# One fused three-block kernel: early expert blocks taken evenly over the experts, dense weights stored by eight blocks, six gathers held, one-hots scaled on ScalarE and GpSimd

## The chip, the cores and the metric

The kernel runs on one core of one Trainium2 chip. The metric is the device time of one execution, in microseconds; lower is better. The engines have names of their own in the trace: PE is TensorE's matmul (PEld its weight load), DVE is VectorE, ACT is ScalarE, POOL is GpSimd, SP is SyncE, which here only issues DMAs.

## The reference, cut to what matters

The program is one transformer-like block (attention and a feed-forward part) followed by a second block whose last part is a product-key mixture of experts. Only that last part is touched. It has 512 tokens of width 1024 and 16384 experts, each a row of `u_tab` and a row of `v_tab`; every token picks 16 experts in each of 8 heads.

```python
def block(hb):
    n = hb.shape[0]
    q = (hb @ w_q).reshape(n, PEER_HEADS, 2, PEER_HALF)
    s = jnp.einsum('nhid,hikd->nhik', q, sub_keys).astype(jnp.float32)
    s_top, i_top = lax.top_k(s, PEER_TOPK)
    cand = s_top[:, :, 0, :, None] + s_top[:, :, 1, None, :]
    cand_idx = i_top[:, :, 0, :, None] * PEER_N_KEYS + i_top[:, :, 1, None, :]
    best, pos = lax.top_k(cand.reshape(n, PEER_HEADS, PEER_TOPK * PEER_TOPK), PEER_TOPK)
    idx = jnp.take_along_axis(cand_idx.reshape(n, PEER_HEADS, -1), pos, axis=-1)
    w = jax.nn.softmax(best, axis=-1)
    u = jnp.take(u_tab, idx, axis=0)
    act = jax.nn.gelu(jnp.einsum('nhkd,nd->nhk', u, hb).astype(jnp.float32))
    out = jnp.einsum('nhk,nhkd->nd', w * act, jnp.take(v_tab, idx, axis=0))
    return out.astype(hb.dtype)
```

## The kernel before, in words

The kernel splits the tokens of this part in two. The first 192 (`NS`) are done as written: 128 expert rows for each token are gathered, a row of `u_tab` is multiplied with the token and summed, a row of `v_tab` is weighted and summed. The other 320 (`ND`) are done densely: for each of 128 *blocks* of 128 experts TensorE multiplies the block's part of `u_tab` with the tokens, ScalarE takes gelu, VectorE multiplies with a matrix W of routing weights that is zero where a token did not pick an expert, and TensorE multiplies with the block's part of `v_tab`. Matrix operands are split in a high and a low half (`split`: ScalarE rounds, VectorE subtracts), and three matmuls make one product (`mm3`, 320 columns each). Weights come in slabs of 1 MB (`raw`, two buffers `wr`, issued by SP), two blocks to a slab of `u_s`.

Three stages in a row are touched.

*Routing* (1700 to 1960 us; the loop `for u in range(16)`). TensorE makes scores (`scores`), VectorE finds the 16 best (`top16`), GpSimd adds candidates (`cd`), and `decode(p)` turns positions into expert numbers for two heads at a time. Beside it TensorE makes 30 *early* blocks (`s_block32`: eight matmuls in plain fp32, then gelu). 38 blocks are early: the first 22 (`NACT`) stay in SBUF, the last 16 (`NSPILL`) go to DRAM (`Sd`) and come back when used.

*One-hots* (1960 to 2104 us; the loop `for sb in range(ND // SB)`, 20 times 16 tokens). For four tokens at a time VectorE compares an iota with the two key numbers (`A`, `B`, tiles of four 128x128 one-hots), `B` is scaled by the routing weights, TensorE multiplies `B` and `A` to the 128x128 matrix of W of each token, and ScalarE copies it to `stg`, which SP stores to DRAM (`Wd`) once for each 16 tokens. In the loop and behind it stand the last early blocks, eight in all.

*Dense* (2104 to 3084 us; the loop `for g in range(NG)`, 32 groups of four blocks). W is loaded for eight blocks at a time (`w_load`). `s_block` makes a fresh block (`pg`, 24 matmuls), `ahead` makes more at a rate of 0.86 a block, so that activations lie some twenty blocks ahead, until block 112, where the spilled ones begin. A group ends in 96 matmuls with `v_s` (`acc`) and eight additions to `x`.

Through all three runs the generator `spa = sparse()`, the work of the first 192 tokens. Each call gathers one row for each of 128 partitions (`rows`, an indirect DMA on GpSimd's queue, seven buffers `ro`), and before that, when three gathers are outstanding (`GLAG`), uses the oldest: a *u row* by a dot product on VectorE (L1337), a *v row* by waiting until four are there and then eight matmuls (`pv`, L1371). 192 u rows and 192 v rows come in the order of `mixed`. It is called 57 times in routing, 20 times in the one-hot stage, and at a rate of 0.82 (`GATHERS`) at 12 places of each group. The order on each engine is that of the code, as a scheduler arranges it; a queue works strictly in its order.

## Time and profile before

| | us |
|---|---|
| median of 3 runs | 3109.74 |
| lowest and highest run | 3103.26, 3118.66 |
| the profiled execution's own time | 3101.83 |
| its span, first to last instruction | 3100.0 |
| PE busy | 2899.0 |
| VectorE busy | 1989.1 |
| ScalarE busy | 1195.9 |
| GpSimd busy | 537.1 |

The runs time the program as a whole; the profile is one execution of it, and the views below are all of that one. Busy times overlap between engines and are a mean over stages with different limits. A busy PE is not PE at its peak, since matmuls are pipelined and their ends are modelled: how many matmul records end in a stretch says more.

### The profile page before, as it was taken

How to read it: one execution, taken by the hardware profiler on the slowest of the kernel's cores; microseconds unless marked ns; L12 is line 12 of the kernel's file. 1: busy time of each engine (PE TensorE's matmuls, PEld its weight loads, DVE VectorE, ACT ScalarE, POOL GpSimd, SP SyncE). 2: the span in 40 equal slices, each digit the busy share in tenths (PEclk: the TensorE clock that was granted, in tenths of full speed). 3: DMA queues.
4: the chain of work that ended last, by engine and by line, in shares of the span. 5: the costliest groups of instructions: out<-in, count | busy, mean ns of one | idle time of the engine just before them, and what ended most of it. 6: DMA issues, size and time to landing. Idle time of an engine off the chain costs nothing.

```text
span 3100.0 us, 43712 instructions
## 1 busy us (share of the span) xinstructions
PE 2899.0 (94%) x17230; PEld 2406.1 (78%) x17230; DVE 1989.1 (64%) x3987; ACT 1195.9 (39%) x1950; POOL 537.1 (17%) x447
## 2 busy tenths in 40 slices
PE   7999999999999999999999997589899989999987
PEld 4786588888898887888887765478888878888866
DVE  4755557554587677444446889997876666654554
ACT  3644445443364433344323110583333333333322
POOL 0000000000000000000000457312434434333332
PEclk9999999999999999999999998799999999999998
DMA  6203422222222232221122558479888888788895
GB/s 239 68 28 115 171 96 83 95 95 95 84 94 96 82 107 75 99 69 55 68 100 73 169 220 300 170 268 317 320 307 307 304 291 293 270 320 310 310 341 215
DMA packets 161806, 551.68 MB, mean 178 GB/s; under 512 B 14512, under 2 KB 70576, under 8 KB 124352
## 3 DMA queue, kind: packets, MB, share of 16 engines
q1 hardware_dynamic: 104416, 343.87, 31.7%
q0 software_dynamic: 55296, 201.35, 18.0%
q10 hardware_dynamic: 1888, 3.66, 0.3%
q8 instruction: 135, 2.21, 0.3%
q14 instruction: 71, 0.58, 0.1%
HBM read 522.98 MB, written 25.82 MB: 177 GB/s over the span
## 4 chain that ended last, share of the span: by engine, by line
PE 72%; DVE 11%; DMA 7%; ACT 4%; issue 3%; POOL 2%; SPq 0%; DVEq 0%; ACTq 0%; POOLq 0%
PE pg L129 15%; PE pg L133 15%; PE pg L132 15%; PE acc L129 4%; PE acc L133 3%; PE acc L132 3%; PE pv L1371 3%; DMA wr<-in_v_s_dram 2%; DMA ro<-in_u_r_dram,idxU 2%; DVE ro L1337 2%; DVE wl L104 2%; PE w L1601 1%; ACT B L1596 1%; ACT stg L1602 1%; PE yq L1041 1%
## 5 line engine op out<-in xcount | busy, mean ns | idle before, releaser
L104 DVE TENSOR_TENSOR wl<-wr,wh 128x1024 fp32r<-128x1024 f32 x446 | 548.9, 1235 | 520.6 <-ACT wh L103 491.5
L129 PE MATMUL pg<-ah,wh 128*128 128x512 f32 (+3 forms) x2472 | 859.4, 348 | 12.2 <-ACT wh L103 4.4
L133 PE MATMUL pg<-ah,wl 128*128 128x512 f32 (+3 forms) x2472 | 852.6, 345 | 8.5 <-DVE wl L104 8.3
L132 PE MATMUL pg<-al,wh 128*128 128x512 f32 (+3 forms) x2472 | 852.4, 345 | 0.0
L103 ACT ACTIVATE wh<-wr 128x1024 fp32r<-128x1024 f32 x446 | 469.2, 1058 | 911.4 <-PE pg L132 467.8
L129 PEld LDWEIGHTS pg<-ah,wh 128*128 128x128 f32 x2472 | 468.6, 190 | 82.7 <-ACT ac L1428 9.3
L133 PEld LDWEIGHTS pg<-ah,wl 128*128 128x128 f32 x2472 | 467.8, 190 | 63.2 <-DVE wl L104 11.7
L132 PEld LDWEIGHTS pg<-al,wh 128*128 128x128 f32 x2472 | 468.6, 190 | 53.1 <-issue 4.0
L129 PE MATMUL acc<-gh,wh 128*128 128x320 f32 x1024 | 325.3, 319 | 38.2 <-DVE x L1678 33.9
L133 PE MATMUL acc<-gh,wl 128*128 128x320 f32 x1024 | 321.2, 315 | 8.4 <-DVE wl L104 8.4
L1328 POOL DMA_INDIRECT ro<-in_u_r_dram,idxU x192 | 251.1, 1308 | 446.9 <-DVE dots L1337 324.2
L132 PE MATMUL acc<-gl,wh 128*128 128x320 f32 x1024 | 321.5, 314 | 0.0
L1337 DVE CUSTOM_DVE_ANT_0 ro<-ro,hT 128x1024 f32<-128x1024 f32 x192 | 234.6, 1249 | 52.6 <-DMA ro<-in_u_r_dram,idxU 52.5
L1328 POOL DMA_INDIRECT ro<-in_v_r_dram,idxV x192 | 208.7, 1087 | 325.1 <-PE pv L1371 239.7
L129 PEld LDWEIGHTS acc<-gh,wh 128*128 128x128 f32 x1024 | 197.2, 193 | 75.6 <-issue 53.3
L133 PEld LDWEIGHTS acc<-gh,wl 128*128 128x128 f32 x1024 | 197.4, 193 | 9.6 <-DVE wl L104 9.5
L1197 POOL MEMSET att<- 128x512 f32 x4 | 2.0, 524 | 1163.6 <-DVE mx L1119 1050.1
L132 PEld LDWEIGHTS acc<-gl,wh 128*128 128x128 f32 x1024 | 197.3, 193 | 0.0
L1441 PE MATMUL pg<-h,wr 128*128 128x320 f32 x608 | 171.7, 438 | 8.0 <-DMA wr<-in_u_s_dram 8.0
L1441 PEld LDWEIGHTS pg<-h,wr 128*128 128x128 f32 x608 | 115.4, 193 | 54.3 <-DMA wr<-in_u_s_dram 8.8
L1678 DVE TENSOR_TENSOR x<-x,acc 128x320 f32<-128x320 f32 x256 | 111.6, 483 | 13.5 <-PE acc L133 12.3
L1601 PE MATMUL w<-A,B 128*128 128x128 f32 x640 | 95.3, 299 | 26.5 <-ACT B L1596 24.5
(570 smaller groups left out, 3892.8 us busy)
## 6 DMA issues: line engine op xcount, KB each, us to landing
wr<-in_u_s_dram SPq DMA_DIRECT2D x64, 1024.0 KB
wr<-in_v_s_dram SPq DMA_DIRECT2D x64, 1024.0 KB
wr<-in_w_in_dram SPq DMA_DIRECT2D x40, 1024.0 KB
wr<-in_w_up_dram SPq DMA_DIRECT2D x22, 1024.0 KB
Wd<-stg SPq DMA_DIRECT2D x20, 1024.0 KB
W<-Wd SPq DMA_DIRECT2D x64, 320.0 KB
wr<-in_ada_w_dram SPq DMA_DIRECT2D x16, 1024.0 KB
wr<-in_w_inA_dram SPq DMA_DIRECT2D x12, 1024.0 KB
```

The lines of the kernel that those rows point to most:

```text
L103: S.activation(hi, src, AF.Copy)
L104: eng.tensor_tensor(lo, src, hi.bitcast(F), op=OP.subtract)
L129: ins = TE.matmul(ps, lh, rh, start=first, stop=False)
L132: TE.matmul(ps, lh, rl, start=False, stop=False)
L133: TE.matmul(ps, ll, rh, start=False, stop=last)
L1041: TE.matmul(pq[:, b * 128 + f * 64:b * 128 + f * 64 + 64], St[:, b * 128:b * 128 + 128], Cf[:, 16 + c * 64:80 + c * 64], start=True, stop= ...
L1328: G.indirect_dma_start(out=t, out_offset=None, in_=a[table], in_offset=bass.IndirectOffsetOnAxis(ap=idx, axis=0))
L1337: yield "u_r", idxU[:, j:j + 1], lambda t, j=j: pin(V.tensor_tensor_reduce(t, t, hx, scale=1.0, scalar=0.0, op0=OP.mult, op1=OP.add, accum ...
L1371: ins = TE.matmul(pv[hf][32 * q:32 * q + 32], sel[:, q], ts[q][:, hf * 512:hf * 512 + 512], start=(i == 0), stop=(i == n - 1))
L1441: TE.matmul(ps, slab[-1][:, c:c + 128], h32[:, k], start=(k == 0), stop=(k == 7))
L1601: last = TE.matmul(ps[:, :, t], B[:, t], A[:, t], start=True, stop=True)
L1678: V.tensor_add(x, x, acc[dc])
```

## The change

The early blocks are no longer the first 22 and the last 16: 19 slabs are taken at even distances over the 64 (`eslab`). The sixteen blocks of the last eight of them are made first and go to DRAM, the 22 others stay in SBUF (`kept`). The dense loop asks `act(n)` for each block, three ahead of use: a kept one, a load, or a fresh one, in small new buffers. `ahead` and the pinned order of its matmuls are gone. The three first rounds of routing make no early block now (26 blocks in routing, seven in the one-hot loop, five behind it; in the order that TensorE gets, one of the seven stands behind too).

`Wd` is laid out by groups of eight blocks, so that a partition's load is one run of 2560 bytes, no longer five of 512; the store in the one-hot stage writes sixteen runs of 512 bytes, formerly one of 8192.

`sparse` uses a row when gathers and held v rows together reach six. Its calls move: 40 in routing, 10 in the one-hot loop, 0.875 a place in the dense loop, and what is left before the last group's matmuls. 20 u rows of the first 128 tokens, not 60, precede those of the other 64, and a round of four v rows has seven u rows, not five.

All of `B` is compared at once. ScalarE scales two of four one-hots, formerly three; GpSimd scales two; VectorE's one fused compare and scale is gone. The last decode runs on VectorE alone, as do the last head's candidate sums.

```diff
-GLAG = 3
-
-GATHERS, SPACE = 0.82, 0.86
+GATHERS = 0.875
...
     def mixed():
         u1, v2 = first(range(128), hT), second(range(128, 192), 128, 16)
-        yield from islice(u1, 60)
+        yield from islice(u1, 20)
         yield from first(range(128, 192), hT2)
         for _ in range(16):
             yield from islice(v2, 4)
-            yield from islice(u1, 5)
+            yield from islice(u1, 7)
...
-            if len(flying) == GLAG:
+            while len(flying) + len(held) >= NRO - 1:
                 t, u = flying.pop(0)
                 u(t)
...
-        Wd = dw.tile([ND // SB, 128, 128, SB], F, name="Wd")
+        Wd = dw.tile([128 // WE, 128, ND // SB, WE, SB], F, name="Wd")
...
-        early = chain(range(128 - NSPILL, 128), range(NACT))
+        def act(n, pool):
+
+            if n in kept:
+                return kept[n]
+            ac = pool.tile([128, ND], F, name="ac", tag="ac")
+            if n in enum:
+                SY.dma_start(ac, Sd[enum[n] - NACT])
+            else:
+                S.activation(ac, gemm_one(ust, hd), AF.Gelu_apprx_tanh)
+            return ac
+
+
+        eslab = [(2 * i + 1) * 64 // (NACT + NSPILL) for i in range((NACT + NSPILL) // 2)]
+        enum = {2 * b + j: 2 * i + j for i, b in enumerate(eslab) for j in range(2)}
+        fresh = [b for b in range(64) if b not in eslab]
+        todo = sorted(enum, key=lambda n: (enum[n] + NSPILL) % (NACT + NSPILL))
...
-                    E = V if p == 3 and b else G
+                    E = V if p == 3 else G
...
-                for _ in range(2 if u < 15 else 0):
+                for _ in range(2 if 2 < u else 0):
                     s_block32()
-                for _ in range(6 if u > 8 else 5 if u > 5 else 0):
+                for _ in range(5 if 5 < u < 14 else 0):
                     next(spa)
...
+                CE = V if hh == 7 else G
...
-                next(spa)
+                if sb % 2:
+                    next(spa)
...
-                    for t in range(3):
+                    for t in (0, 1):
                         S.activation(B[:, t], B[:, t], AF.Copy, scale=wl(t))
-                    V.tensor_scalar(B[:, 3], iot, i2T[:, t0 + 3:t0 + 4], wl(3), op0=OP.is_equal, op1=OP.mult)
+                        G.tensor_scalar(B[:, t + 2], B[:, t + 2], wl(t + 2), None, op0=OP.mult)
...
-                SY.dma_start(Wd[sb], stg)
-                if sb % 5 == 1 and len(acts) < NACT - 4:
+                SY.dma_start(Wd[:, :, sb].rearrange("g p e t -> p g e t"), stg.rearrange("p (g e) t -> p g e t", e=WE))
+                if sb % 3 == 1 and len(todo) > 4:
...
-                SY.dma_start(Wn[-1][:, c], Wd[c, :, n:n + WE].rearrange("s p e t -> p s e t"))
+                SY.dma_start(Wn[-1][:, c], Wd[n // WE, :, c])
...
-                    while len(acts) <= min(n + 2, 127):
-                        if len(acts) < 128 - NSPILL:
-                            s_block()
-                        else:
-                            s_load()
+                    while len(acts) <= min(n + 3, 127):
+                        acts.append(act(len(acts), pact2))
...
-                    ahead()
+                if g == NG - 1:
+                    for _ in spa:
+                        pass
```

The order of instructions shows what the diff alone does not, at three places. The first is TensorE at the end of routing, where the early blocks (`pg` from `wr`) stand ahead of the transposes of the expert numbers (`i1T`, `i2T`, `wT`). Before:

```order
L1441 MATMUL pg<-h_13137,wr 128x320 x2
L1490 MATMUL sc<-skT,qT 128x128 x4
L1441 MATMUL pg<-h_13137,wr 128x320 x62
L1581 MATMUL i1T<-con,i_13446 128x128 x4
L1581 MATMUL i2T<-con,i_13447 128x128 x4
L1581 MATMUL wT<-con,ww 128x128 x4
```

And now:

```order
L1452 MATMUL pg<-h_13137,wr 128x320 x2
L1496 MATMUL sc<-skT,qT 128x128 x4
L1452 MATMUL pg<-h_13137,wr 128x320 x78
L1590 MATMUL i1T<-con,i_13446 128x128 x4
L1590 MATMUL i2T<-con,i_13447 128x128 x4
L1590 MATMUL wT<-con,ww 128x128 x4
```

Sixteen more of these matmuls, two blocks, lie between the last scores and the transposes, though routing has four blocks fewer in all.

The second place is the one-hot loop. VectorE before, for four tokens and the next dot product (L1337):

```order
L1592 TENSOR_TENSOR A<-iot,i1T 128x512
L1592 TENSOR_TENSOR B<-iot,i2T 128x384
L1597 TENSOR_SCALAR B<-iot,i2T,wlT 128x128
L1592 TENSOR_TENSOR A<-iot,i1T 128x512
L1592 TENSOR_TENSOR B<-iot,i2T 128x384
L1597 TENSOR_SCALAR B<-iot,i2T,wlT 128x128
L1337 ISA ro,dots<-ro,hT 128x1024
```

VectorE now:

```order
L1602 TENSOR_TENSOR B<-iot,i2T 128x512
L1602 TENSOR_TENSOR A<-iot,i1T 128x512
L1602 TENSOR_TENSOR B<-iot,i2T 128x512
L1602 TENSOR_TENSOR A<-iot,i1T 128x512
L1602 TENSOR_TENSOR B<-iot,i2T 128x512
L1333 ISA ro,dots<-ro,hT_13130 128x1024
```

GpSimd's queue from the last decode on, before:

```order
L1328 DMA ro<-in_u_r_dram,idxU 128x1024 x5
L1515 TENSOR_TENSOR eq<-eq,tb 128x2048
L1517 TENSOR_TENSOR eq<-eq 128x8x128
L1517 TENSOR_TENSOR eq<-eq 128x8x64
L1517 TENSOR_TENSOR eq<-eq 128x8x32
L1518 TENSOR_TENSOR i_13446<-eq 128x4x32
L1328 DMA ro<-in_u_r_dram,idxU 128x1024 x64
```

And now:

```order
L1559 TENSOR_TENSOR cd<-tv 128x4x64
L1561 TENSOR_TENSOR cd<-tv 128x4x48
L1324 DMA ro<-in_u_r_dram,idxU 128x1024
L1607 TENSOR_SCALAR B<-B,wlT 128x128 x8
L1324 DMA ro<-in_u_r_dram,idxU 128x1024
L1607 TENSOR_SCALAR B<-B,wlT 128x128 x16
L1324 DMA ro<-in_u_r_dram,idxU 128x1024
```

VectorE loses the fused instruction and compares all four of `B`; GpSimd's decode is gone, and its queue takes 160 scalings between the gathers, sixteen to a gather.

The third place is TensorE at the very end, the last `pv` groups and the transposes of their sums (`vo`). Before:

```order
L133 MATMUL acc<-gh,wl 128x320
L1371 MATMUL pv<-ro,sel 32x512 x8
L1384 MATMUL vo<-con,vo 128x128 x4
L129 MATMUL acc<-gh,wh 128x320
L132 MATMUL acc<-gl,wh 128x320
L1384 MATMUL vo<-con,vo 128x128 x4
L133 MATMUL acc<-gh,wl 128x320
```

And now:

```order
L129 MATMUL pg<-ah,wl 128x320
L1371 MATMUL pv<-ro,sel 32x512 x24
L1384 MATMUL vo<-con,vo 128x128 x8
L127 MATMUL acc<-gh,wh 128x320
L128 MATMUL acc<-gl,wh 128x320
```

Three groups of v rows now stand together ahead of the last group's 96 matmuls; before, the last two had 45 `acc` matmuls between them, and 51 stood behind the last.

## Rows read from the trace of the kernel before

**Rows 1.** Stretches: length, busy us (records) of each engine, clock, DMA share, GB/s.

```profile
1700.00:1960.00 260.00, 209.10 (x834) 154.68 (x833) 228.57 (x890) 32.62 (x55) 153.06 (x110) 0.90 0.60 215
1960.00:2104.00 144.00, 117.52 (x728) 99.42 (x727) 130.13 (x281) 119.78 (x328) 22.97 (x21) 0.95 0.66 238
2104.00:2150.00 46.00, 40.74 (x221) 35.65 (x221) 33.67 (x61) 14.78 (x25) 10.99 (x9) 0.96 0.98 321
2150.00:2300.00 150.00, 135.44 (x891) 132.49 (x891) 128.76 (x213) 53.14 (x76) 62.87 (x48) 0.94 0.89 319
2300.00:2700.00 400.00, 372.13 (x2449) 339.96 (x2449) 264.76 (x427) 131.84 (x187) 155.75 (x121) 0.97 0.83 299
2700.00:2900.00 200.00, 199.61 (x1395) 172.95 (x1393) 104.27 (x171) 68.92 (x97) 60.68 (x61) 1.00 0.83 304
2900.00:3000.00 100.00, 89.38 (x599) 73.72 (x598) 52.91 (x94) 28.52 (x40) 39.88 (x37) 0.96 0.91 332
3000.00:3084.00 84.00, 79.62 (x528) 61.08 (x522) 41.18 (x76) 23.96 (x33) 27.25 (x28) 0.99 0.72 254
```

**Rows 2.** Groups by line and form, 1700 to 1960: busy us, mean ns, idle before.

```profile
L1441 PE MATMUL pg<-h,wr 128*128 128x320 f32 x476 | 135.1, 440 | 8.0 <-DMA wr<-in_u_s_dram 8.0
...
L1337 DVE CUSTOM_DVE_ANT_0 ro<-ro,hT 128x1024 f32<-128x1024 f32 x54 | 68.9, 1322 | 9.6 <-DMA ro<-in_u_r_dram,idxU 9.5
```

**Rows 3.** Waits, 1700 to 1960: who waited for whom, us, times, longest.

```profile
PE i1T L1581 <- POOL i L1518: 33.5, 1, 33.5
```

**Rows 4.** Timeline, VectorE and GpSimd, 1723 to 1741: start, duration, instruction.

```profile
1723.37 1.21 DVE L1514 TENSOR_TENSOR eq<-io16b,ab 128x2048 bf16<-128x2048 bf16 x1
1724.66 3.65 POOL L1515 TENSOR_TENSOR eq<-eq,tb 128x2048 bf16<-128x2048 bf16 x1 [10.50 <-DVE eq L1514]
1724.92 4.47 DVE L1514 TENSOR_TENSOR eq<-io16b,ab 128x2048 bf16<-128x2048 bf16 x1
...
1740.73 0.81 POOL L1518 TENSOR_TENSOR i<-eq 128x128 f32<-128x128 bf16 x2
```

**Rows 5.** Groups by line and form, 1960 to 2104.

```profile
L1596 ACT ACTIVATE B<-B,wlT 128x128 f32<-128x128 f32 x240 | 78.0, 391 | 2.7 <-DVE B L1592 2.4
L1592 DVE TENSOR_TENSOR A<-iot,i1T 128x512 f32<-128x512 f32 x80 | 55.0, 687 | 7.7 <-PE w L1601 5.9 <-PE wT L1581 1.7
L1602 ACT ACTIVATE stg<-w 128x512 f32<-128x512 f32 x80 | 47.7, 596 | 15.0 <-PE w L1601 14.9
L1592 DVE TENSOR_TENSOR B<-iot,i2T 128x384 f32<-128x384 f32 x80 | 44.2, 553 | 0.0
L1597 DVE TENSOR_SCALAR B<-iot,i2T,wlT 128x128 f32<-128x128 f32 x80 | 29.4, 367 | 0.0
L1337 DVE CUSTOM_DVE_ANT_0 ro<-ro,hT 128x1024 f32<-128x1024 f32 x20 | 24.4, 1220 | 0.0
```

**Rows 6.** DMA view, 2106.5 to 2110.5, almost only W loads.

```profile
DMA packets 2448, 1.22 MB, mean 306 GB/s; under 512 B 61, under 2 KB 2448, under 8 KB 2448
```

**Rows 7.** DMA view, 2102 to 2104, almost only 8 KB packets.

```profile
DMA packets 103, 0.79 MB, mean 393 GB/s; under 512 B 7, under 2 KB 7, under 8 KB 7
```

**Rows 8.** DMA view, 2104 to 3085; gathers are the software queue, 303 of them.

```profile
DMA packets 103694, 297.73 MB, mean 303 GB/s; under 512 B 7881, under 2 KB 50889, under 8 KB 89673
...
q0 software_dynamic: 43632, 158.88, 44.1%
```

**Rows 9.** Waits, 2104 to 3085.

```profile
POOL ro L1328 <- PE pv L1371: 324.3, 48, 15.9
...
DVE ro L1337 <- DMA ro<-in_u_r_dram,idxU: 43.0, 14, 8.9
```

**Rows 10.** Chain that ended last: start, us, what; first and last of four, and v.

```profile
2301.09 9.41 DMA ro<-in_u_r_dram,idxU
...
2653.93 10.81 DMA ro<-in_u_r_dram,idxU
...
3039.53 5.26 DMA ro<-in_v_r_dram,idxV
```

More of the change, by code (lines that the diff above doesn't have):

```diff
@@ L126, in half, with mm3 @@
         return wh, wl
-    def mm3(ps, lh, ll, rh, rl, first, last, hold=False):
-        ins = TE.matmul(ps, lh, rh, start=first, stop=False)
-        if hold:
-            tc.keep_in_program_order(ins)
+    def mm3(ps, lh, ll, rh, rl, first, last):
+        TE.matmul(ps, lh, rh, start=first, stop=False)
         TE.matmul(ps, lh, rl, start=False, stop=False)
@@ L155, in next, with gemm_one @@
             return self.h[0][:, c], self.h[1][:, c]
-    def gemm_one(st, X, meta=False, hold=False):
+    def gemm_one(st, X, meta=False):
         if meta:
@@ L170, in gemm_one @@
                 xh, xl = xh[:, 16:], xl[:, 16:]
-            mm3(ps, wh, wl, xh, xl, k == 0, k == len(X) - 1, hold and k == 0)
+            mm3(ps, wh, wl, xh, xl, k == 0, k == len(X) - 1)
         return ps
@@ L1338, in first @@
                 t, t, hx, scale=1.0, scalar=0.0, op0=OP.mult, op1=OP.add, accum_out=dots[:, j:j + 1]))
+    held = []
     def second(js, at, n):
         c = slice(js[0], js[-1] + 1)
-        st = {"ts": []}
+        st = {}
         def begin():
@@ L1350, in begin @@
             else:
-                for q in (slice(0, 64), slice(64, 128)):
-                    TE.matmul(ps[q], dots[q, c], ident[q, q], start=True, stop=True)
+                for q in range(4):
+                    h, m = slice(q % 2 * 64, q % 2 * 64 + 64), js[0] + q // 2 * 32
+                    TE.matmul(ps[32 * q:32 * q + 32], dots[h, m:m + 32], ident[h, h], start=True, stop=True)
             gT = gg.tile([128, 4 * n], F, name="gT", tag=f"gT{n}")
@@ L1360, in use @@
                 begin()
-            ts, pv = st["ts"], st["pv"]
+            ts, pv = held, st["pv"]
             ts.append(t)
@@ L1420, in tile_kernel @@
     with tc.tile_pool(name="dw", bufs=1, space=bass.MemoryType.DRAM) as dw, tc.tile_pool(name="act", bufs=NACT) as pact:
-        Wd = dw.tile([ND // SB, 128, 128, SB], F, name="Wd")
+        Wd = dw.tile([128 // WE, 128, ND // SB, WE, SB], F, name="Wd")
         Sd = dw.tile([NSPILL, 128, ND], F, name="Sd")
-        ust = Stream(a["u_s"][NACT // 2:64 - NSPILL // 2])
         acts, slab = [], []
-        def s_block(pool=None, hold=False):
-            ac = (pool or pact).tile([128, ND], F, name="ac", tag="ac")
-            S.activation(ac, gemm_one(ust, hd, hold=hold), AF.Gelu_apprx_tanh)
-            acts.append(ac)
-        early = chain(range(128 - NSPILL, 128), range(NACT))
+        def act(n, pool):
[11 more added lines that the diff above has]
+        todo = sorted(enum, key=lambda n: (enum[n] + NSPILL) % (NACT + NSPILL))
+        kept = {}
+        ust = Stream([a["u_s"][b] for b in fresh])
         def s_block32():
-            n = next(early)
+            n = todo.pop(0)
             if n % 2 == 0:
@@ L1443, in s_block32 @@
             S.activation(ac, ps, AF.Gelu_apprx_tanh)
-            if n < NACT:
-                acts.append(ac)
-            else:
-                SY.dma_start(Sd[n - 128 + NSPILL], ac)
-        def s_load():
-            ac = pact.tile([128, ND], F, name="ac", tag="ac")
-            SY.dma_start(ac, Sd[len(acts) - 128 + NSPILL])
-            acts.append(ac)
+            if enum[n] < NACT:
+                kept[n] = ac
+            else:
+                SY.dma_start(Sd[enum[n] - NACT], ac)
         tt = ctx.enter_context(ExitStack())
@@ L1522, in decode @@
                 k1, k2 = (x[:64, 1, hs].rearrange("p h k -> p (h k)") for x in (i1, i2))
-                d = idxU[:64, 128 + 32 * p:160 + 32 * p] if p < 2 else idxM[:, 32 * p - 64:32 * p - 32]
-                V.scalar_tensor_tensor(d, k1, 128.0, k2, op0=OP.mult, op1=OP.add)
-                if p == 3:
-                    S.dma_start(idxU[64:, 128:], idxM)
+                m = slice(p // 2 * 32, p // 2 * 32 + 32)
+                c = slice(128 + m.start, 128 + m.stop)
+                V.scalar_tensor_tensor(idxM[:, m] if p % 2 else idxU[:64, c], k1, 128.0, k2, op0=OP.mult, op1=OP.add)
+                if p % 2:
+                    SY.dma_start(idxU[64:, c], idxM[:, m])
                 yield
@@ L1608, in tile_kernel @@
             with tc.issue_after(last.ins):
-                while len(acts) < NACT:
+                while todo:
                     s_block32()
@@ L1612, in tile_kernel @@
         hst.close()
-        with tc.tile_pool(name="gg", bufs=1) as gg, tc.tile_pool(name="w3", bufs=1) as w3:
+        with tc.tile_pool(name="act2", bufs=4) as pact2, tc.tile_pool(name="gg", bufs=1) as gg, tc.tile_pool(name="w3", bufs=1) as w3:
             halves["more"] = w3
-            due = {"g": 0.0, "s": 0.0}
+            due = [0.0]
             def feed():
-                due["g"] += GATHERS
-                while due["g"] >= 1:
-                    due["g"] -= 1
+                due[0] += GATHERS
+                while due[0] >= 1:
+                    due[0] -= 1
                     next(spa, None)
-            def ahead():
-                due["s"] += SPACE
-                if due["s"] >= 1 and len(acts) < 128 - NSPILL:
-                    due["s"] -= 1
-                    s_block(pact, True)
             Wn = []
```

15 lines of the change are left out of this document (8 added, 7 removed).

## The prediction

> **What bounds the kernel now.** I read the stretch view first, cut at the borders of the last three stages; the first 1700 us hold nothing that the change touches. The *routing* (1700 to 1960 us) keeps VectorE busy 228.6 of 260 us, TensorE 209 and the DMA engines 0.60. The *one-hot* stage (1960 to 2104) keeps VectorE busy 130 of 144, ScalarE 120, TensorE 118. The *dense* stage (2104 to 3084) is TensorE's: 199.6 of 200 us between 2700 and 2900, where it finishes 1395 matmul records, 0.143 us each [rows 1]. I take that as its best pace here. The other dense stretches are worth, at that pace, 38 us of 46 (221 records, of which 49 are the fp32 kind at about 0.27), 127 of 150, 350 of 400, 86 of 100 and 76 of 84. So 102 of the 980 us are not work: 8, 23, 50, 14 and 8 in order of time, nothing between 2700 and 2900. That lost time is what a better order can win, and by stretch it lies mostly where u rows and v rows are gathered in turn (2300 to 2700).
>
> **A, routing.** `spa` is advanced 57 times here before and 40 times after, and the use of a row lags its gather by 3 before, by 6 after. So 54 dot products on VectorE become 34. Each costs 68.9/54 = 1.28 us [rows 2] plus 0.08 for its accumulator: 20 x 1.36 = 27 us less. The last decode's first half moves from GpSimd to VectorE: one multiply over 128x2048 and three adds. No row shows it undisturbed; a VectorE compare of that size alone takes 1.21 us, the GpSimd multiply 3.65 [rows 4], so the half lies between two of the first (2.4) and two of the second (7.3); I take 5. Against that the second compare, which sat out a GpSimd multiply (4.47 against 1.21 us), no longer does: 3.3 back. The two cd sums on VectorE I take at nothing, since GpSimd made VectorE wait for them too; their upper bound is the two GpSimd durations, about 1 us. Sum: -27 + 5 - 3 = -25. TensorE must not become late: the order puts 78 fp32 matmuls ahead of the transposes of i1, formerly 62, 16 more at 2 x 135.1/476 = 0.57 us, 9 us. TensorE waited 33.5 us there for the decode [rows 3], and 33.5 - 25 - 9 leaves nothing to spare but is not negative. **I take -24**; bounds -30 and -12 (the later half of the saving eaten by gather or weight waits).
>
> **B, one-hot stage.** VectorE's rows sum to 55.0 + 44.2 + 29.4 for the one-hots and 24.4 for the dots [rows 5], 153 us of durations that overlap to 130 busy, factor 0.85. After: two full compares, 55.0 + 55.0, and ten dots, 12.2: 122 x 0.85 = 104 us. ScalarE: 160 scalings of 240, 52 + 47.7 = 100. TensorE: 117.5 busy with four blocks in the loop; three more at 8 x 0.57 = 4.5 us make 131 with its present gaps. So without GpSimd the stage would end some 8 to 20 us earlier, on TensorE. But GpSimd now does 160 multiplies of 128x128 with one tensor input. The nearest row is its add over 128x128, two inputs, 0.81 us for two, 0.40 each [rows 4]. And the same rows show that the two engines shut each other out: VectorE's compare that began at 1724.92 ended at 1729.39; less its 1.21 it ran from 1728.18, 0.13 before GpSimd's recorded end. Of 0.40 us at most 0.27 would then block; below, 0.15 for a one-input form that is mostly overhead. The compares here read two SBUF tensors (iota and index), so they meet it. 160 x 0.15 to 0.40 is 24 to 64 us on VectorE: 128 to 168 against 130. I take 0.17: 131, near what TensorE needs. The Trainium skill (SBUF — State Buffer, section "Who interferes with whom") has this as a rule: a VectorE instruction with two SBUF inputs and a GpSimd instruction that reads SBUF exclude each other for the whole instruction. Rows 4 agree for the instruction's body, not for its last 0.13 us; by the rule in full, with 0.40 us each, VectorE would need 168 us.
>
> The stores of Wd go from 8 KB to 512 B pieces. A stretch of W loads alone, in 512 B packets, ran at 306 GB/s [rows 6]; slabs in 8 KB packets at 393 [rows 7]. A 1 MB slab then takes 3.4 us, not 2.7: 20 x 0.76 = 15 us of transfer, hidden behind a share of 0.66 of 144 us, and ten gathers leave the stage. If that cover went, +15. **I take -3 for B**; bounds -20 and +38 (168 for VectorE's 130).
>
> **C, dense stage.** Its terms:
> - *Two more fp32 blocks after the last one-hot* (48 matmuls for 32): 16 x 0.57 = +9 on TensorE, at the stage's head where TensorE is the busy engine.
> - *Gathers that VectorE waited for.* VectorE waited 43.0 us, 14 times, for u rows [rows 9]; the chain passes through such a landing four times, 9.41 us the first, 10.81 the last, 39 together [rows 10]. In a round of four v and five u rows the fourth u row takes a buffer that only the pv matmuls free, and its dot follows four calls of `spa` later; with six held it follows seven calls later. At 0.875 per feed and 12 feeds a group of some 31 us a call is 3 us, so the row gains about 9 us, the size of those waits. All 39 would be the bound, 0 the other; I take half, -20.
> - *Even blocks.* The 22 us lost after 2900 are in groups without u blocks, where TensorE outruns its transfers; spread, they have other matmuls to do. 0 to -22; I take -11.
> - *Transfers.* 27 gathers move in (77 + 4 gone before 2104, 50 + 4 after); a gather is 158.88 MB/303 = 0.52 MB [rows 8], so +14.2 MB, at 303 to 332 GB/s +43 to +47 us of transfer. W in 2560 B packets saves up to 21 MB at 306 against 393 GB/s, 15 us. Net +28 to +32 on DMA engines that are 0.72 to 0.98 busy. Hidden where TensorE is full; I take +5, the bounds are 0 and +32. The Trainium skill (DMA: Bandwidth & Descriptors, section "Specifications") puts line rate at 512 B and above. By that the layout would change nothing in either stage; rows 6 and 7 differ (306 and 393), and the measurement decides.
> - *The end.* The order puts three pv groups back to back, then the transposes, then 96 acc matmuls; before, acc matmuls lay between them. The gathers of these rows then have nothing in front of them. The last such wait cost 5.26 [rows 10]; two of them uncovered, +10; bounds 0 and +20.
>
> Sum: 9 - 20 - 11 + 5 + 10 = **-7**, bounds about -50 and +40.
>
> **Sum.** -24 - 3 - 7 = -34. The profiled execution took 3101.83 us, so 3068; the median of the runs shown is 7.9 us above it, so **3076 us**.
>
> **Rivals.**
> 1. *Six in flight is already seven.* GpSimd's queue runs ahead of program order: it stood 324 us waiting for pv matmuls to free a buffer [rows 9], so seven buffers, not `GLAG`, set how many gathers fly. The new rule then only delays the uses. Against it: the delay is just what VectorE's waits lack. Without the -20 the sum is -14: 3096 us. Chance 0.16.
> 2. *GpSimd shuts VectorE out in full.* B becomes +38, the sum +7: 3117. For it rows 4; against it that those multiplies have two inputs and 16 times the elements. Decides from 0.27 us of blocking for each. Chance 0.12.
> 3. *Transfers bound the dense stage (slower).* It moved 297.73 MB at a mean of 303 GB/s [rows 8]; with 311.9 MB at that rate it takes 1029 us instead of 980, +49, and the sum is -24 - 3 + 49 = +22: 3132. For it: shares of 0.83 to 0.98, and TensorE starved in the very stretches where they are highest. Against it: 332 GB/s between 2900 and 3000, and a full TensorE at 304. It decides where the stage cannot pass 318 GB/s (311.9 MB in 980 us). Chance 0.11.
>
> **Numbers.** Forecast 0.55, rivals 0.16, 0.12, 0.11, and 0.06 for a dense stage that wins nearly all of its lost time (-50 in place of -7: 3033). About half a per cent, 15 us, is what a measurement of this kernel can tell from no change. The forecast and the last case are faster; rival 1 lies at the border and is parted, rival 2 is no change, rival 3 slower. Faster 0.66, no change 0.22, slower 0.12. The range from 3030 to 3118 leaves out rival 3 and what lies past the last case.
>
> **What would show it.** Right: dots between the routing's start and the first compare 34, and that stage some 24 us shorter; compares of about 0.69 us with few stretched ones and a one-hot stage within 10 us of its 144; no wait of VectorE for u rows above 10 us in all; TensorE's records above 6.5 per us in the mixed stretch. Wrong: compares stretched by GpSimd's multiplies (rival 2), the same VectorE waits (rival 1), ScalarE waiting longer for weight slabs with DMA shares above 0.9 throughout (rival 3), or TensorE waiting for activations now that blocks are made three ahead instead of some twenty. I price that last wait at nothing: gelu, product and the two halves are four instructions of about half a us each behind 48 or more matmuls, 7 us.

## The result, and the profile after

The changed kernel takes **3150.41 us** (median of 4 runs, 3146.52 to 3158.86) against 3113.62 of the kernel before on the same chip (4 runs): ratio 1.0126, 95% interval 1.009 to 1.0162. It is 1.3% slower, clear of the interval; forecast were 3076 us and a range from 3030 to 3118. Its profiled execution took 3148.71 us (span 3146.9), 46.9 more than the 3101.83 of before. The medians differ by 36.8 only: before's profiled execution lies 11.8 us below its median, the changed kernel's 1.7, so the stretches below add up to some 10 us more than the medians do.

Five marks in the trace tell where: the first transpose of `i1`, the last one-hot matmul, the first product with W, the last sum into x, and the end. The table gives the us from mark to mark, for every kernel of this study; stretches of one program differ by up to 8 us from trace to trace (the dense stage is one program in after, e1 and e2; the way to i1T is one in e14 and e17), so a smaller difference is read only where the medians bear it out.

```
kernel          to i1T one-hot to W dense  tail |  median   ratio to before (95%)
before          1958.6  141.2  12.5  970.8 17.0 | 3113.62
after           1920.8  183.8  32.2  994.3 16.0 | 3150.41  1.0126 [1.0090, 1.0162]
e1              1924.8  142.1  32.8  993.2 16.0 | 3110.09  0.9993 [0.9974, 1.0012]
e2              1918.8  139.6  32.5 1001.6 16.0 | 3111.94  0.9991 [0.9975, 1.0008]
e3              1922.3  185.1  14.0 1011.9 16.5 | 3149.86  1.0114 [1.0089, 1.0138]
e4              1921.0  182.9  13.6 1011.8 15.8 | 3152.14  1.0130 [1.0104, 1.0156]
e5              1919.8  147.9  32.3  976.6 16.0 | 3090.78  0.9944 [0.9924, 0.9963]
e6              1922.0  142.1  33.0  975.0 16.4 | 3087.78  0.9935 [0.9914, 0.9956]
e7              1960.0  143.4  12.5  957.0 16.6 | 3098.89  0.9959 [0.9939, 0.9978]
e8              1942.4  135.5  11.8  985.4 16.6 | 3096.35  0.9956 [0.9932, 0.9979]
e9              1936.7  133.8  11.8  994.7 20.5 | 3105.27  0.9976 [0.9957, 0.9995]
e10             1925.6  145.4  32.8  985.4 16.1 | 3105.62  0.9985 [0.9967, 1.0004]
e11             1919.4  183.3  33.8  982.0 16.1 | 3132.41  1.0074 [1.0046, 1.0101]
e12             1950.7  148.5  23.0  978.8 16.1 | 3122.02  1.0032 [1.0016, 1.0049]
e13             1919.2  144.1  32.1  972.1 15.8 | 3095.20  0.9941 [0.9919, 0.9964]
e14             1928.5  144.1  32.5  967.1 16.4 | 3090.56  0.9937 [0.9913, 0.9960]
e15             1946.7  143.0  32.4  951.5 17.0 | 3091.43  0.9929 [0.9905, 0.9954]
e16             1959.0  193.9  12.2  971.4 16.3 | 3155.60  1.0137 [1.0096, 1.0179]
e17             1920.4  145.1  32.6  977.5 17.0 | 3090.28  0.9921 [0.9889, 0.9952]
e18             1953.1  146.6  12.9  949.7 16.8 | 3080.47  0.9894 [0.9865, 0.9923]
```

Routing 37.8 us shorter, one-hots 42.6 longer, head and dense stage together 983.3 before and 1026.5 after, 43.2 longer. The stretches of after, at the cuts of [rows 1]:

```profile
1960.00:2104.00 144.00, 114.90 (x612) 98.32 (x612) 95.65 (x145) 79.29 (x204) 133.60 (x142) 0.81 0.58 175
2104.00:2150.00 46.00, 41.39 (x185) 33.04 (x184) 13.86 (x22) 11.54 (x20) 2.90 (x3) 0.93 0.60 217
2150.00:2300.00 150.00, 132.46 (x871) 127.29 (x870) 124.48 (x210) 49.37 (x70) 69.41 (x53) 0.94 0.86 320
2300.00:2700.00 400.00, 360.11 (x2334) 331.40 (x2333) 295.00 (x483) 128.30 (x180) 169.49 (x137) 0.96 0.86 320
2700.00:2900.00 200.00, 190.77 (x1289) 164.69 (x1289) 114.45 (x197) 65.79 (x93) 72.42 (x67) 0.98 0.84 312
```

In the one-hot stage the busy engine is now GpSimd (133.60 of 144 us); VectorE, ScalarE and TensorE are all less busy than in [rows 1], and TensorE's granted clock is 0.81, not 0.95. In the dense stage TensorE finishes fewer records in each stretch up to 2900 and more in the two behind it (632 against 599, 577 against 528). The stage's groups, 1921 to 2105, as in [rows 5]:

```profile
L1607 POOL TENSOR_SCALAR B<-B,wlT 128x128 f32<-128x128 f32 x160 | 152.1, 966 | 45.7 <-DVE B L1602 38.5 <-PE w L1611 6.9
L1611 PE MATMUL w<-A,B 128*128 128x128 f32 x640 | 113.5, 341 | 40.1 <-POOL B L1607 24.5 <-ACT B L1606 15.4
L1602 DVE TENSOR_TENSOR A<-iot,i1T 128x512 f32<-128x512 f32 x80 | 58.7, 733 | 56.2 <-PE w L1611 50.9 <-issue 5.3
L1602 DVE TENSOR_TENSOR B<-iot,i2T 128x512 f32<-128x512 f32 x80 | 56.5, 707 | 0.0
L1612 ACT ACTIVATE stg<-w 128x512 f32<-128x512 f32 x80 | 47.5, 594 | 66.6 <-PE w L1611 66.6
```

The compares are hardly longer than before (733 against 687 ns for `A`). VectorE sits idle 56.2 us, 50.9 of them for TensorE, and TensorE in its turn waits mostly for GpSimd (24.5 of 40.1 us). A scaling takes 0.966 us in the mean. What stretches it stands in the timelines of GpSimd and then VectorE, 2006 to 2014 (some rows of the second):

```profile
2005.68 2.33 POOL L1607 TENSOR_SCALAR B<-B,wlT 128x128 f32<-128x128 f32 x4
2008.18 1.02 POOL L1324 DMA_INDIRECT ro<-in_u_r_dram,idxU  x1 [0.17 <-issue]
2009.23 5.18 POOL L1607 TENSOR_SCALAR B<-B,wlT 128x128 f32<-128x128 f32 x4
...
2007.50 0.82 DVE L1602 TENSOR_TENSOR A<-iot,i1T 128x512 f32<-128x512 f32 x1 [2.27 <-PE w L1611]
...
2009.45 0.68 DVE L1602 TENSOR_TENSOR B<-iot,i2T 128x512 f32<-128x512 f32 x1
2010.05 0.77 DVE L1602 TENSOR_TENSOR A<-iot,i1T 128x512 f32<-128x512 f32 x1
2010.74 0.68 DVE L1602 TENSOR_TENSOR B<-iot,i2T 128x512 f32<-128x512 f32 x1
2011.35 0.77 DVE L1602 TENSOR_TENSOR A<-iot,i1T 128x512 f32<-128x512 f32 x1
2012.04 0.68 DVE L1602 TENSOR_TENSOR B<-iot,i2T 128x512 f32<-128x512 f32 x1
```

While VectorE idled before 2007.50, four scalings took 2.33 us, 0.58 each; while it compared without a break, four took 5.18, 1.3 each. That is one scaling to two compares. VectorE lost little by it: from 2009.45 on its compares start 0.60 to 0.69 us apart, and one in two takes 0.77 and not 0.68.

At the dense stage's head six fp32 blocks stand behind the last one-hot, and SP, holding slab loads for them, comes late to W. Chain, 2080 to 2180:

```profile
2104.70 25.86 PE pg L1452 x96
2132.41 4.29 DMA W<-Wd
```

and the waits of the dense stage, 2105 to 3132:

```profile
ACT gh L101 <- DVE ac L1658: 113.3, 63, 9.3
PE acc L127 <- DVE x L1680: 48.2, 15, 7.3
...
DVE ro L1333 <- DMA ro<-in_u_r_dram,idxU: 34.5, 9, 7.6
```

VectorE's wait for u rows fell from 43.0 us [rows 9] to 34.5 only, and its products and sums are late for ScalarE and TensorE.

### The profile page after: what moved, and what is told of

The parts are those of the page before. It is cut to its first block, busy times and chain, and to the rows that moved or that the text cites. A ratio compares the mean times of both kernels' runs of the same rounds, so it can differ in the third digit from the quotient of the medians.

```text
span 3146.9 us, 43817 instructions
## 1 busy us (share of the span) xinstructions
PE 2941.9 (93%) x17234; PEld 2435.4 (77%) x17234; DVE 1987.7 (63%) x3914; ACT 1177.3 (37%) x1870; POOL 667.1 (21%) x600
## 5 line engine op out<-in xcount | busy, mean ns | idle before, releaser
L127 PE MATMUL acc<-gh,wh 128*128 128x320 f32 x1024 | 326.6, 320 | 48.8 <-DVE x L1680 48.2
L1324 POOL DMA_INDIRECT ro<-in_u_r_dram,idxU x192 | 241.1, 1256 | 275.7 <-DVE dots L1333 195.8
L1607 POOL TENSOR_SCALAR B<-B,wlT 128x128 f32<-128x128 f32 x160 | 152.1, 966 | 45.7 <-DVE B L1602 38.5
L1611 PE MATMUL w<-A,B 128*128 128x128 f32 x640 | 113.5, 341 | 40.1 <-POOL B L1607 24.5
```

The source lines that it names most:

```text
L127: TE.matmul(ps, lh, rh, start=first, stop=False)
L1324: G.indirect_dma_start(out=t, out_offset=None, in_=a[table], in_offset=bass.IndirectOffsetOnAxis(ap=idx, axis=0))
L1607: G.tensor_scalar(B[:, t + 2], B[:, t + 2], wl(t + 2), None, op0=OP.mult)
L1611: last = TE.matmul(ps[:, :, t], B[:, t], A[:, t], start=True, stop=True)
```

## The experiments

Theory 1: GpSimd bounds the one-hot stage by its scalings. Theory 2: W waits on SP's queue. Theory 3: the blocks spread evenly, or else the gathers, lengthen the dense stage. Later numbers arose from results. Times are in the table above.

### The one-hots: e1, e2, e16

**e1** gives the changed kernel the old scaling:

```diff
-                    for d, src in ((A, i1T), (B, i2T)):
...
+                    for d, src, n in ((A, i1T, 4), (B, i2T, 3)):
...
-                    for t in (0, 1):
+                    for t in range(3):
                         S.activation(B[:, t], B[:, t], AF.Copy, scale=wl(t))
-                        G.tensor_scalar(B[:, t + 2], B[:, t + 2], wl(t + 2), None, op0=OP.mult)
+                    V.tensor_scalar(B[:, 3], iot, i2T[:, t0 + 3:t0 + 4], wl(3), op0=OP.is_equal, op1=OP.mult)
```

> The changed kernel with the one-hot scaling of before: ScalarE scales three of the four one-hots of a group, VectorE compares and scales the fourth in one instruction, GpSimd scales none. Theory 1 (GpSimd's 160 scalings of 0.97 us are the bound of the one-hot stage): from the first transpose of i1 to the last one-hot matmul 184 us become 135 to 145, and the kernel ends 40 us earlier, at about 3110 us. Rival (the stage grew from its three more fp32 blocks and from the stores of Wd in 512 B pieces): the stage stays above 165 us and the kernel above 3130.

The stage fell to 142.1 us, the kernel to 3110. **e2** leaves one scaling of four on GpSimd:

```diff
-                    for t in (0, 1):
+                    for t in range(3):
                         S.activation(B[:, t], B[:, t], AF.Copy, scale=wl(t))
-                        G.tensor_scalar(B[:, t + 2], B[:, t + 2], wl(t + 2), None, op0=OP.mult)
+                    G.tensor_scalar(B[:, 3], B[:, 3], wl(3), None, op0=OP.mult)
```

> The changed kernel with three one-hots of a group scaled by ScalarE and one by GpSimd, so 80 scalings on GpSimd and not 160. Theory 1 (GpSimd's own duration bounds the stage; VectorE is hardly blocked by it): 80 x 0.97 = 78 us fit behind VectorE, the stage returns to 140 to 150 us and the kernel to 3110 to 3115 us. Rival (each scaling shuts VectorE out for its duration): half of the loss stays, a stage of about 162 us and a kernel of about 3130.

Stage 139.6, kernel 3112. GpSimd's row of e2, 1919 to 2058:

```profile
L1607 POOL TENSOR_SCALAR B<-B,wlT 128x128 f32<-128x128 f32 x80 | 101.6, 1283 | 53.4 <-DVE B L1602 38.3 <-PE w L1611 14.7
```

Its mean rose to 1.283 us, for VectorE now compares nearly without a break, and yet the stage is as short as in before: the two engines do disturb each other, and it is GpSimd that pays. **e16** puts the new scaling alone into the kernel before:

> The kernel before with the changed kernel's one-hot scaling alone (ScalarE two, GpSimd two of a group, VectorE compares all four). Theory 1 (GpSimd, 160 scalings of 0.97 us, is the bound of the stage, whatever else the kernel does): from the first transpose of i1 to the last one-hot matmul 141 us become 180 to 190, the kernel 3155 us. Rival (it takes the changed kernel's extra fp32 blocks and its stores in 512 B pieces too): under 165 us, and a kernel below 3140.

Stage 193.9 (180 to 190 was expected), the whole kernel 3155.60; the changed kernel's blocks and stores have no part in it. From 1960 to 2153 of e16, GpSimd was busy 182.24 of 193 us, VectorE 131.38, with a clock of 0.74:

```profile
1960.00:2153.00 193.00, 147.48 (x714) 126.78 (x714) 131.38 (x203) 98.16 (x247) 182.24 (x181) 0.74 0.50 172
```

Theory 1 holds.

### Head and dense stage: e3, e4, e6, e7

**e3** moves the first W loads ahead of the trailing fp32 blocks:

```diff
-            with tc.issue_after(last.ins):
-                while todo:
-                    s_block32()
...
             for q in range(4):
                 w_load(0, q)
+            with tc.issue_after(last.ins):
+                while todo:
+                    s_block32()
```

> The changed kernel with the first eight W loads ahead of the trailing fp32 blocks in the program, so that on SP's queue they stand ahead of those blocks' slab loads. Theory 2 (W waited on SP behind slab loads whose buffers the fp32 blocks held): the gap from the last one-hot matmul to the first W product goes from 32 us to about 12, and the kernel ends 12 to 20 us earlier, at 3130 to 3138 us. Rival (TensorE has the 48 matmuls of the trailing blocks to do in that time anyway, and takes up the dense work no earlier): under 6 us gained, 3145 or more.

The gap fell from 32.2 to 14.0 us, and the dense stage grew by 17.6: nothing gained, theory 2 falls. TensorE had the 96 records of the blocks to do in either order. **e4** takes the early blocks of before:

```diff
-        eslab = [(2 * i + 1) * 64 // (NACT + NSPILL) for i in range((NACT + NSPILL) // 2)]
+        eslab = [*range(NACT // 2), *range(64 - NSPILL // 2, 64)]
...
-                    while len(acts) <= min(n + 3, 127):
-                        acts.append(act(len(acts), pact2))
+                    while len(acts) <= min(n + 2, 127):
+                        acts.append(act(len(acts), pact))
...
+                    ahead()
```

> The changed kernel with the early blocks of before: the first 22 and the last 16 experts, dense blocks made ahead into freed buffers by SPACE 0.86, the pair that keeps program order restored; gathers, Wd layout and one-hots stay as changed. Theory 3a (spread blocks made three ahead leave ScalarE waiting for the W product, 113 us, and TensorE with it): the dense stage from the first W product to the last x add goes from 994 us to about 970, and the kernel to about 3125 us. Rival 3b (the dense stage grew by the 27 gathers and dots that moved into it): the stage stays within 5 us of 994, and the kernel within 8 us of 3150.

Head and dense stage were 1025.4 us against 1026.5: which blocks are early and how far ahead they are made does nothing here. ScalarE's waiting for products goes down with it only from 113.3 to 93.6 us. **e6** loads W for the first 16 blocks only and leaves the other loads out, on e1 (what follows calls blocks experts):

```diff
             def w_load(n, q):

+                if n >= 2 * WE:
+                    if q == 0:
+                        Wn.append(Wn[-2])
+                    return
```

> The run with the old one-hot scaling (3110 us), in which W is loaded for the first 16 experts only and used again for all later ones, so the products of the other 112 experts are not the right ones: 56 loads of 0.33 MB, 18.4 MB, are left out of the dense stage. Theory 4 (its transfers set the dense stage): 18.4 MB at 306 GB/s are 60 us, head and dense stage 1026 down to 966 and the kernel to about 3050. Rival (gathers one by one, their latency and the order around them, or TensorE's work set it): less than 15 us gained, 3095 or more.

Of 60 us 18 came (1026.0 to 1008.0). Head and dense stage, first of e1 and then of e6:

```profile
2067.00:3093.00 1026.00, 948.74 (x6121) 835.16 (x6119) 662.31 (x1098) 326.24 (x459) 385.41 (x333) 0.96 0.83 308
```

```profile
2064.00:3073.00 1009.00, 943.87 (x6122) 831.00 (x6120) 663.39 (x1099) 325.92 (x459) 391.51 (x333) 0.97 0.80 295
```

They moved 315.60 MB at 308 GB/s in e1 and 297.34 MB at 295 in e6: the rate fell with the load, so a fixed rate of bytes is not the bound. Only W's bytes were taken out; the gathers' 174.61 MB stayed, and what a limit on these alone would do e6 does not test. **e7** puts the new layout of Wd alone into the kernel before:

> The kernel before with the new layout of Wd alone (stores in 512 B pieces, loads in 2560 B pieces). Theory 4: the loads of W, 21 MB, go at up to 393 and not 306 GB/s, up to 15 us less transfer in the dense stage, of which some 10 are seen, and the stores hide in the one-hot stage: 3100 to 3107 us. Rival (a transfer's bytes count, not the size of its pieces): within 5 us of the kernel before.

Nearly the whole of the 15 us that I had allowed the layout: head and dense stage 983.3 to 969.5; the one-hot stage, with its smaller stores, is 2 us longer, within the spread.

### The gathers: e5, e8, e9, e10, e11, e15

**e5** is e1 with a call in every one-hot stage, ten gathers fewer in the dense stage:

```diff
-                if sb % 2:
-                    next(spa)
+                next(spa)
```

> The run with the old one-hot scaling (3110 us) with a gather call in each of the 20 stages of the one-hot loop, not in every second, and so ten gathers fewer in the dense stage (0.85 of a call per feed). Theory 4 (the head and the dense stage together last as long as their transfers, 315.6 MB at 306 GB/s: in five kernels they were 1025 to 1034 us whatever stood first): ten gathers of 0.52 MB less are 5.2 MB, 17 us, and the ten dots hide in the one-hot stage, where VectorE is busy 121 of 142 us: 3093 us. Rival (a gather and its dot cost the same wherever they stand): the one-hot stage grows by 12 us and the kernel stays above 3104.

3090.78 us: 17 us off the dense stage for some 6 in the one-hot stage. That is the number of theory 4, whose reason e6 refutes. **e8** and **e9** give the kernel before the changed kernel's calls:

```diff
-                for _ in range(6 if u > 8 else 5 if u > 5 else 0):
+                for _ in range(5 if 5 < u < 14 else 0):
...
+                if sb % 2:
+                    next(spa)
```

> The kernel before with the changed kernel's number of gather calls alone: 40 in the routing (57), one in every second one-hot stage (20 became 10), 0.875 of a call per feed (0.82), so 27 more gathers in the dense stage; three in flight as before. Theory 4: the routing ends 18 to 24 us earlier, the dense stage lasts 27 x 0.52 MB / 303 GB/s = 46 us longer, and the kernel 3135 us. Rival 3b' (the dense stage of the changed kernel grew by its even blocks, its six in flight or its end, not by the number of gathers): the dense stage grows by less than 15 us, and the kernel ends below 3110.

> The kernel before with the changed kernel's number of gather calls alone, as in the run before it, but at 0.885 of a call per feed, so that the last gather is used too (in that run the calls ended one short, and the use of the last 128 tokens' v rows, their transposes and sums were left out). Theory 5 (a gather in the dense stage costs some 1.66 us there, 17 us for ten, in some other way than by its bytes, since 18.4 MB of W taken out gave only 18 us): head and dense stage go from 983 to 983 + 27 x 1.66 = 1028 us, and with 16 us less in the routing and 6 in the one-hot stage the kernel ends at about 3133 us. Rival 5b (the slope of the run before, 14 us for 27): about 997 to 1005 us and a kernel of 3095 to 3108.

e8 left the last use out, so e9 counts: routing 21.9 us shorter, one-hots 7.4 shorter, head and dense stage 23.2 longer (27 gathers, 0.86 us each), near rival 5b. **e10** takes six in flight back from e5:

```diff
-            while len(flying) + len(held) >= NRO - 1:
+            if len(flying) == 3:
```

> The run with ten more calls in the one-hot stage (3091 us) with the rule of before for using a gathered row: three calls after it was asked for, not as late as the seven buffers allow. Theory 6 (the later uses gave nothing, since the buffers and not the rule set how many gathers fly, and made rows wait longer for their use): head and dense stage 1009 go down by 10 us or more, the kernel to 3080 or less. Rival 6b (six in flight saves VectorE's waits for u rows, 20 us as forecast): the kernel goes up to 3105 or more. Between them, 3085 to 3097: the rule does nothing.

Head and dense stage 9 us longer, routing 6: six in flight is worth something, and theory 6 falls; 3105.62 is just the number of rival 6b. **e11** makes two calls in each one-hot stage:

> The same base (3091 us) with two gather calls in each of the 20 stages of the one-hot loop (40 in place of 20) and 0.80 of a call per feed, so 20 gathers fewer in the dense stage. Theory 5: 20 x 1.66 = 33 us less in the dense stage, and 12 to 20 us more in the one-hot stage, whose VectorE has about 20 of 148 us free: 3072 to 3079 us. Rival 5b: the dense stage gains 10 to 12 us, the one-hot stage loses 24: 3100 or more.

A miss on both counts: the one-hot stage took 183.3 us, 35 more than e5, and the dense stage gained nothing from 20 fewer gathers (1015.8 against 1008.9). Two stretches of e11, early and later in its one-hot stage:

```profile
1950.00:1970.00 20.00, 15.79 (x105) 13.45 (x104) 20.00 (x42) 16.48 (x44) 7.86 (x6) 1.00 0.92 271
...
2030.00:2050.00 20.00, 15.80 (x69) 13.84 (x70) 18.47 (x39) 13.44 (x38) 5.24 (x4) 0.66 0.80 263
```

First VectorE is full, then TensorE's granted clock falls from 1.00 to 0.66, and the same 15.8 busy us hold 69 records and not 105. **e15** has before's order of gathers and its 57 and 20 calls, on e5; **e14** only the order:

```diff
-        yield from islice(u1, 20)
+        yield from islice(u1, 60)
...
-            yield from islice(u1, 7)
+            yield from islice(u1, 5)
```

> The same base (3091 us) with the order of gathers of before (60 u rows first, then rounds of four v and five u, in place of 20 and rounds of four and seven), with as many calls as the base at each place. Theory 9 (the longer mixed phase, 16 rounds of 11 in place of 14 of 9, costs what is not yet accounted for in the dense stage, some 15 us): 3075 to 3082 us. Rival 9b (the order does nothing): 3086 to 3096 us.

> The run with the old order of gathers, and with before's 57 calls in the routing (40) and 0.82 of a call per feed (0.85), so 307 gathers in the dense stage as before. Theory 10 (in the changed kernel's dense stage 17 gathers cost 15 to 28 us, as ten cost 17 and 27 cost 23): against that run the head and dense stage are 15 to 28 us shorter and the routing 20 to 24 longer, the kernel within 8 us of it. Rival 10b (the ten gathers' 17 us came from the rhythm of the calls, not their number: twenty more gave nothing): the dense stage gains under 8 us and the kernel ends 12 us or more later than that run.

The order does nothing in sum (3090.56). Against e14, 17 gathers fewer shorten head and dense stage by 15.7 us and move the mark at the routing's end by 18.2. The routing itself grew by more, 26 us: in e14 its first top-16 search starts at 1697.3, in e15 at 1688.7, for a reason that lies in the stages before. By the medians (3090.56 and 3091.43) it is an exchange, as theory 10 has it.

### The end and the blocks' places: e13, e17, e12

**e13** is e5, and **e17** is e14, without the emptying:

```diff
-                if g == NG - 1:
-                    for _ in spa:
-                        pass
```

> The base with 20 calls in the one-hot stage (3091 us) without the emptying of the gathers ahead of the last group's matmuls: 0.87 of a call per feed, so that the last rows are used in the last group's feeds, between its matmuls. Theory 8 (the last three pv groups back to back, with their landings, the transposes and the sums, stand ahead of the last group's 96 matmuls: that group takes 34 to 37 us in every kernel that has this and 18 to 21 in those that do not): the last group takes about 20 us and the kernel 3075 us. Rival 8b (the last group is longer since it is one of those with u blocks, or since its work is only moved behind the last x sum): 3086 us or more.

> The changed kernel with the old one-hot scaling, 20 calls in the one-hot stage, the old order of gathers and no emptying ahead of the last group (0.87 of a call per feed): the kernel that gave 3091 us with both single edits. Theory 8 (the emptying costs 4 to 14 us, the rest is paid back in the groups before): 3078 to 3086 us. Rival 8b: 3088 us or more.

The last group went from 34 to 23 us in e13, but neither kernel is faster than its partner: the work came earlier, and theory 8 falls. **e12** puts the fp32 blocks of e5 back to their places:

```diff
-                for _ in range(2 if 2 < u else 0):
+                for _ in range(2 if u < 15 else 0):
...
-                if sb % 3 == 1 and len(todo) > 4:
+                if sb % 5 == 1 and len(todo) > 4:
```

> The same base (3091 us) with the fp32 blocks placed as before: two in each of the routing's first 15 steps (26 became 30), one in every fifth one-hot stage (it was every third), four behind the last. Theory 7 (two more blocks behind the last one-hot cost 9 us at the dense stage's head, three more in the loop 5 us there): 3077 us. Rival 7b (TensorE, 197 of 225 us busy in the end of the routing, has no room for four more blocks there): the routing ends 9 to 18 us later and the kernel stays at 3088 or above.

The gap to W is 9.3 us shorter, and the routing 30.9 us longer. Where from, the routing's stretches show, first of e12 and then of after:

```profile
1700.00:1951.00 251.00, 208.12 (x843) 154.84 (x842) 201.90 (x864) 33.44 (x55) 114.86 (x85) 0.92 0.50 179
```

```profile
1700.00:1921.00 221.00, 194.92 (x780) 144.64 (x779) 201.44 (x864) 31.12 (x49) 114.81 (x85) 0.94 0.53 189
```

VectorE does the same 864 instructions in the same 201 busy us; e12 lets it idle 49 us and after 20. By the wait view it does not idle for the scores (0.2 us in e12), but for ScalarE's halves of the weights `w_q` of which the scores are made (15.7 us, 1.1 in after), for gathered rows (12.2 and 4.3) and for the decodes (12.2 and 7.2); ScalarE waited 35.2 us for slabs of `w_q`, 12.5 in after.

### The best found: e18

**e18** is the kernel before with the Wd layout and the later use of rows:

```diff
-            if len(flying) == GLAG:
+            while len(flying) + len(held) >= NRO - 1:
```

> The kernel before with the two edits that single runs showed to gain: the new layout of Wd (-12 us) and the later use of rows, as late as seven buffers allow (-9 in the dense stage of the changed kernel); 57 and 20 calls as before, 0.825 of a call per feed so that all rows are used. Theory 6b (the later use saves VectorE's waits for u rows whatever the order): 3088 us, a dense stage of 948. Rival 6 (in the kernel before the buffers, not the rule, already set what is in flight): 3097 or more.

**3080.47 us**, ratio 0.9894 (0.9865 to 0.9923): faster than both kernels. VectorE's wait for u rows, 43.0 us in [rows 9] and 36.2 in e7, is 9.5 here:

```profile
DVE ro L1337 <- DMA ro<-in_u_r_dram,idxU: 9.5, 2, 5.8
```

## Why the prediction was wrong

**B and C failed, each by more than the whole forecast of -34.** For B -3 was forecast, +42.6 came, past the upper bound of +38; e1, e2 and e16 show the cause. The failed step is "I take 0.17": I priced what GpSimd's scaling would block on VectorE, and from an add of 0.40 us. I never laid GpSimd's own sum beside the stage; at 0.40 us it would have been 64 us and no warning, so it is the price beside a busy VectorE that was missing. Alone a scaling takes 0.58 us, beside compares 1.3; 160 of them are 152 us, more than the 141 of the stage before, while VectorE's compares stayed at 0.71 to 0.73 us. Rival 2 had the size (+38) and the wrong side: GpSimd is held up, not VectorE. The Trainium skill (SBUF — State Buffer, section "SBUF: two separate sides") has a VectorE instruction with two SBUF inputs and a GpSimd instruction that reads SBUF exclude each other for the whole instruction. Here the trace does not agree: by it, the four scalings of 0.58 us would have taken 2.3 of the 5.2 us from a VectorE that compared without a break and lost some 0.09 to each. The rows of before had shown it [rows 4] for a longer GpSimd multiply with two inputs only.

**A was mis-sized, in my favour.** -24 forecast, -37.8 measured. The sign was right by its reason: VectorE's busy time up to the first transpose fell as forecast, from 228.6 of 260 us [rows 1] to 201.4 of 221; the other 12 us are idle time, 31 down to 20, which had no term. The calls alone gave -21.9 (e9; I had 27 for the dots) and left the idle time as it was, 31 of 237 us:

```profile
1700.00:1937.00 237.00, 204.65 (x826) 151.99 (x825) 206.04 (x854) 32.75 (x53) 134.26 (x94) 0.94 0.56 200
```

The decode on VectorE, for which I had +5 and -3, gained 4: from the last top-16 search to the transposes all six kernels with the old decode took 15.2 us and all fourteen with the new one 11.4 (single traces, within 0.02 us of each other). TensorE did not become late; it still waited 3.2 us ahead of the transposes (my 33.5 - 25 - 9 is not "not negative" but -0.5). Where the rest of the idle time went is open. Putting the blocks back costs 30.9 us in e12, all of it idle, but e9 has its blocks at those places too and idles 18 us less: e12 shows that the places matter in the changed kernel, not what the move was worth.

**C: -7 forecast, +43.2 measured.** The failed step is "Hidden where TensorE is full; I take +5". The bounds were added wrong as well: the upper bounds of the terms make +61, not +40. Term by term:
- *Two more fp32 blocks, +9*: about right, 9.3 in the gap to W and 7 in head and dense stage together (e12).
- *Gathers that VectorE waited for, -20*: the mechanism is right (43.0 to 9.5 us of waits in e18), the size was half or less: 9 us of the stage in the changed kernel (e10; 15 between the medians, routing included), 7 in that of before (969.5 to 962.6, e7 to e18; 18 between the medians). Rival 1 is refuted.
- *Even blocks, -11*: nothing (e4).
- *Transfers, +5*: the layout's 15 us were right (13.8, e7). But 27 gathers cost 23 us in the kernel before (e9), and in the changed one 33, 17 for the ten from e1 to e5 and 16 for the 17 from e14 to e15. Rival 3 came nearest the stage's length (1029 us), by a mechanism that e6 refutes: 18.4 MB less gave 18 us, not 60.
- *The end, +10*: in the last group, but paid back (e13, e17).

What a gather costs beside its bytes was not isolated; a fixed time for each is not it, for e1 did 333 in the 1026 us of head and dense stage, and e11 303 in 1016. The longer waits of TensorE for VectorE's sums (48.2 against 33.9 us before) fit a dot of 1.22 us that stands ahead of them on VectorE, which is argued, not shown. Two things stay open: e15's head and dense stage last as long as before's (983.9 and 983.3), though by the single runs the layout, the later use and the blocks should leave it some 12 us shorter; and e11's gained nothing from 20 fewer gathers. The first may in part lie in which execution was profiled, for by the medians e15 is 22 us faster than before and by the two traces only 10; against that, e16's trace, which lies at its median, has the same stage of before in 983.6 us. The place of the W loads on SP's queue, which I had not priced, cost nothing (e3).

Routing and dense stage nearly exchange gathers one for one, so with the old one-hots the rest of the change is a draw (e1: 0.9993): 34 us won in the routing, 43 lost behind it.

## What to carry over

Before work goes to an idle engine, lay that engine's own sum beside the stage, with the price of the instruction while its neighbour is at work, not only what it does to the neighbour. Work moved from a stage into the next is a gain only if the next has room: here 17 gathers left the routing and ten the one-hots, and of the 29 us that this gave there (e9) the dense stage took 23 back. Of a bundle, single edits tell what to keep: two of this one's, alone in the kernel before, make it 1.1% faster.

## What was not expected of the hardware

GpSimd's scaling of 128x128 f32 took 0.592 us at least, 0.794 in the median and 1.861 at most, and the VectorE compares of `B` 0.677 to 0.856: GpSimd paid nearly the whole price of their working side by side. In the stretch shown it got through one scaling to two compares, and VectorE gave up some 0.09 us to each; a hold for the whole scaling would have cost VectorE some 0.6.

TensorE's granted clock moved with it. Two stretches of 20 us, first of e1's one-hot stage and then of after's:

```profile
1975.00:1995.00 20.00, 18.27 (x121) 15.51 (x120) 18.31 (x40) 18.26 (x51) 1.15 (x1) 1.00 0.82 257
```

```profile
2010.00:2030.00 20.00, 15.04 (x75) 12.31 (x74) 14.86 (x23) 11.84 (x32) 19.80 (x21) 0.83 0.53 158
```

In e1 TensorE kept the upper of its two levels (2.4 GHz); in after, where it idled between groups for GpSimd, it had a mixture of the two, and was busy 113.5 us with the 640 one-hot matmuls that took 94.2 in e1. How much of the 42 us the clock holds, no run parts from GpSimd's own 19.8 of 20 busy us.
